# A second drain on GpSimd's queue, behind its last transfer, in a copy kernel

## The chip, the cores and the metric

The kernel runs on one core of a Trainium2 chip. The metric is the device time of one execution in microseconds (us), and lower is better. Three executions of the kernel before took 744.84, 744.95 and 745.9 us; their median, 744.95 us, is the time before.

Three of the core's engines matter here, and they matter through their queues of instructions: SyncE (SP in the profile), ScalarE (ACT) and GpSimd (POOL). Each of them issues DMA transfers. TensorE and VectorE (PE, DVE) have no work but to take part in the barriers at the two ends of the program. A name with a q behind it (POOLq, SPq) means an instruction that the engine's sequencer handles, such as a wait, a semaphore update or a drain.

## The reference

The reference cuts overlapping windows out of each sequence of a batch. Nothing is computed: every output element is a copy of an input element.

```python
batch, length, dim = x.shape                      # 32, 4096, 256, float32
n_windows = (length - window_size) // stride + 1  # 64, 32 -> 127
for i in range(n_windows):
    start = i * stride
    result[:, i] = x[:, start:start + window_size].copy()
```

The output is (32, 127, 64, 256) float32. Since the stride is half the window, each block of 32 rows (32 x 256 floats, 32 KB) goes to two places: it is the first half of one window and the second half of the window before it.

## The kernel before

The kernel is made of DMA transfers alone. The program calls a 32 KB block `blk`; a sequence has 128 of them, and 127 windows of two blocks.

There are two ways for a sequence. Eleven of the 32 (every third, from the second on) are *staged* by `Staging`: ScalarE's queue loads the 128 blocks into a tile in SBUF, one block for each partition, and stores the tile twice, once to the first halves of the windows and once to the second halves. There are six tiles; six sequences are loaded and stored, and then the other five use the same tiles again. The other 21 sequences are *direct*: transfers from DRAM to DRAM copy 16 windows at a time, issued by SyncE's queue (`windows`, line 34 in the profile). Whether a turn is one transfer of 1 MB or two of 512 KB is settled by the sum kept in `share`.

What is left over are the `edges`: 15 windows at one end of each direct sequence (4 for the last one), that don't fill a block of 16. GpSimd's queue issues them. It first waits on the semaphore `near` (line 192), which one of SyncE's last transfers raises, and then, for each edge, for the stores of the staged neighbours in `place` (lines 194 to 196). In the trace, 18 of these transfers are issued one after the other from 654.39 us on, and three more from 702.01 us. Behind them, line 200 issues one last transfer of GpSimd by `columns` (line 44 in the profile): nine windows of sequence 30, cut into sixteenths of a block so that it consists of 4 KB pieces. Then SyncE waits for the stores of the last staged sequence, and issues a small transfer of the same kind (line 202), at 729.80 us.

The semaphores `done`, `near`, `rest` and `ended` count what has landed. SyncE's queue waits for each of them in lines 204 and 205; GpSimd's transfers of lines 197 and 200 are counted in `rest`. No line of the kernel makes GpSimd wait for its own transfers.

All of this stands inside one `with tc.tile_critical()` (line 172). When that block is left, the program appends instructions of its own, shown under line 172: SyncE raises a semaphore; SyncE, ScalarE and GpSimd each run a DRAIN that waits for it and raises a semaphore in turn; and SyncE waits for these three before it goes on. At the end of the whole program (line 236, where the `TileContext` is left) there follow two barriers over all five engines, again made of DRAIN and EVENT_SEMAPHORE instructions, with a clearing of the semaphores on GpSimd's queue between them.

The instructions of one queue are handled in the order in which they stand in it. The queue of GpSimd from line 200 on therefore reads: the last transfer, the DRAIN of line 172, the instructions of line 236.

Of the kernel before, what the change touches and what calls it, by code (L numbers as in the profile page):

```python
# [125 lines left out]
@with_exitstack  # L126
def kernel(
    ctx: ExitStack,
    tc: tile.TileContext,
    x: bass.AP,  # L130
    window_size: bass.AP,
    stride: bass.AP,
    out: bass.AP,
):
    nc = tc.nc
    W, S = int(window_size), int(stride)
    B, L, D = x.shape
    n_win = (L - W) // S + 1
    assert out.shape == (B, n_win, W, D)
    c = Copier(x, out, B, L, D, W, S, n_win)  # L140


    staged = [*range(1, B, 3)]
    items = [(b, -1 if b == B - 1 else 0, c.nb) for b in staged]
    place = {b: g for g, (b, _, n) in enumerate(items) if n == c.nb}
    direct = [b for b in range(B) if b not in staged]
    pool = ctx.enter_context(tc.tile_pool(name="xb", bufs=1))
    st = Staging(c, tc, pool, x.dtype, items, 6)
    ring_d, ring_s, ring_r = nc.sync, nc.scalar, nc.gpsimd
    done = tc.alloc_semaphore("done")  # L150
    near = tc.alloc_semaphore("near")
    rest = tc.alloc_semaphore("rest")
    total = {done: 0, near: 0, rest: 0}

    def count(dma, sem):
        dma.then_inc(sem, 16)
        total[sem] += 16

    sixteens = []
    for b in direct:
        w = 15 if b - 1 in staged else 0
        sixteens += [(b, w + 16 * j) for j in range((c.nw - w) // 16)]
    singles = [(B - 1, c.nw - 1, 1)]
    edges = [(b, 0 if b - 1 in staged else 112, 15) for b in direct[:-1]]
    last = B - 2
    edges.append((last, 112, 4))

    first_loads, loads, stores = 6 * 17, 5 * 17, 6 * 34  # L170
    turns = share = 0
    with tc.tile_critical():  # L172
        st.run(ring_s)

        for i, (b, w) in enumerate(sixteens):
            sem = near if i == len(sixteens) - 2 else done
            second = turns - first_loads - stores
            loading = turns < first_loads or 0 <= second < loads
            share += 120 if turns < 16 or -8 <= second < 16 else 90 if loading else 18
            if share >= 120:  # L180
                share -= 120
                turns += 4
                count(c.windows(ring_d, b, w, 16, 0), done)
                count(c.windows(ring_d, b, w, 16, 1), sem)
            else:
                turns += 3
                count(c.windows(ring_d, b, w, 16), sem)
            if i == len(sixteens) // 2:
                for b, w, half in singles:
                    count(c.windows(ring_d, b, w, 1, half, 2048), done)  # L190

        ring_r.wait_ge(near, 16)
        for b, w, n in edges:
            for k in (b - 1, b + 1):
                if k in place and b != last:
                    st.wait_stored(ring_r, place[k])
            count(c.windows(ring_r, b, w, n), rest)


        count(c.columns(ring_r, last, 116, 9), rest)  # L200
        st.wait_stored(ring_d, place[B - 1])
        count(c.columns(ring_d, last, 125, 2), done)
        total[st.ended] = st.count[st.ended]
        for sem, n in total.items():
            ring_d.wait_ge(sem, n)
# [35 lines left out]
```

## Time and profile before

| what | value |
|---|---|
| median of three executions | 744.95 us (744.84 to 745.9) |
| profiled execution: its time, from its first to its last instruction | 749.4 us (no other figure is given for it) |
| that span over the median | 4.45 us, 0.6% |
| bytes moved by DMA, mean rate | 313.26 MB, 418 GB/s |
| transfers issued by SyncE, ScalarE, GpSimd | 204, 41, 22 |
| busy time of GpSimd | 12.8 us of 749.4 |
| issue of GpSimd's last transfer | 703.7 us, lasting 581 ns |
| start of the closing of line 172 | 746.6 us |
| last instruction of the program | 749.4 us |

Times in the profile count from the first instruction. A row of a line's instructions has the engine, the operation and how often it occurs, then the shortest, the median and the longest duration in nanoseconds, and then when the first and the last of them started. A row of waits has who waited, on whom, the time in total, how often, and the longest. A row of windows has the stretch, its length, the busy time of GpSimd with its number of instructions, the granted clock of TensorE, the share of the 16 DMA engines in use, and the rate in GB/s.

### The profile page before, as it was taken

The numbers are of one execution on the slowest core, as the hardware profiler recorded it, in microseconds if no ns is written. First come the engines' busy times: TensorE is split into PE (matmuls) and PEld (weight loads), VectorE is DVE, ScalarE is ACT, GpSimd is POOL, SyncE is SP. The second block draws the span as 40 slices with busy tenths as digits, with TensorE's granted clock in tenths as the row PEclk, the third lists the DMA queues.
The fourth block names the chain that finished last, engine by engine and source line by source line (L and its number), as shares of the span: only waits on it lengthen the run. The fifth ranks groups of instructions, "written<-read, shape, count | busy, mean of one in ns | idle before, by whom it ended". The sixth has DMA issues, their size and how long they took to land.

```text
span 749.4 us, 322 instructions
## 1 busy us (share of the span) xinstructions
POOL 12.8 (2%) x26
## 2 busy tenths in 40 slices
POOL 0000000000000000000000000000000000040100
DMA  8999999999999999999999999999999999999996
GB/s 360 401 427 429 427 429 428 434 423 418 420 424 423 418 424 415 422 427 427 414 427 417 429 432 429 430 422 430 429 423 421 423 421 419 425 426 423 431 409 262
DMA packets 18290, 313.26 MB, mean 418 GB/s; under 512 B 4336, under 2 KB 4336, under 8 KB 4528
## 3 DMA queue, kind: packets, MB, share of 16 engines
q1 hardware_dynamic: 8016, 154.32, 48.8%
q10 hardware_dynamic: 9104, 138.41, 44.0%
q0 software_dynamic: 1168, 20.51, 6.5%
q14 instruction: 2, 0.02, 0.0%
HBM read 220.95 MB, written 267.09 MB: 651 GB/s over the span
## 4 chain that ended last, share of the span: by engine, by line
another core or an unknown queue 92%; POOL 2%; issue 0%; POOLq 0%; SPq 0%
POOL out_dram L34 2%; POOL out_dram L44 0%; POOLq L236 0%; SPq L172 0%; POOLq L114 0%
## 5 line engine op out<-in xcount | busy, mean ns | idle before, releaser
L34 POOL DMA_DIRECT2D out_dram<-in_x_dram x21 | 12.0, 576 | 691.3 <-DMA out_dram<-in_x_dram 654.0
L44 POOL DMA_DIRECT2D out_dram<-in_x_dram x1 | 0.6, 581 | 0.0
L222 POOL MEMSET const-float32-0.0<- 128x1 f32 x1 | 0.1, 98 | 0.2 <-issue 0.2
L222 POOL MEMSET const-bfloat16-1.0<- 128x1 bf16 x1 | 0.1, 101 | 0.0
L222 POOL MEMSET const-float32-1.0<- 128x1 f32 x1 | 0.1, 98 | 0.0
L222 POOL MEMSET const-uint8-127<- 128x1 uint8 x1 | 0.1, 98 | 0.0
## 6 DMA issues: line engine op xcount, KB each, us to landing
out_dram<-in_x_dram SPq DMA_DIRECT2D x92, 1024.0 KB, 100.7
out_dram<-xb ACTq DMA_DIRECT2D x21, 4096.0 KB, 139.7
out_dram<-in_x_dram SPq DMA_DIRECT2D x110, 512.0 KB, 90.3
xb<-in_x_dram ACTq DMA_DIRECT2D x10, 4096.0 KB, 131.4
out_dram<-in_x_dram POOLq DMA_DIRECT2D x20, 960.0 KB, 38.5
xb<-in_x_dram ACTq DMA_DIRECT2D x4, 1024.0 KB, 15.7
out_dram<-xb ACTq DMA_DIRECT2D x2, 1024.0 KB, 113.4
out_dram<-xb ACTq DMA_DIRECT2D x4, 512.0 KB, 96.9
```

The lines of the kernel that those rows point to most:

```text
L34: return q.dma_start(out=self.oap((b * self.nw + w0) * 2 + h, [[2 * blk, n], row]), in_=self.xap(b * self.nb + w0 + h, [[blk, n], row]), m ...
L44: return q.dma_start(out=self.oap((b * self.nw + w0) * 2, [[part, 16], [2 * self.blk, n], row]), in_=self.xap(b * self.nb + w0, [[part, 16 ...
L222: nc = _bacc.Bacc("TRN2", target_bir_lowering=False, num_devices=1)
```

## The change

One instruction is added to GpSimd's queue, between its last transfer (line 200) and whatever the end of the critical block appends. It waits on no semaphore and raises none. Nothing else is changed: the transfers, their order on each queue, and all waits stay.

```diff
         count(c.columns(ring_r, last, 116, 9), rest)
+        ring_r.drain()
         st.wait_stored(ring_d, place[B - 1])
         count(c.columns(ring_d, last, 125, 2), done)
         total[st.ended] = st.count[st.ended]
```

The queue of GpSimd then reads: the last transfer, the new DRAIN, the DRAIN of line 172, the instructions of line 236. The two lines below the new one are SyncE's.

## The prediction

> **What bounds the kernel now.** I read the page first: how busy the DMA engines are and who moves the bytes.
>
> ```profile
> DMA  8999999999999999999999999999999999999996
> ...
> q1 hardware_dynamic: 8016, 154.32, 48.8%
> q10 hardware_dynamic: 9104, 138.41, 44.0%
> q0 software_dynamic: 1168, 20.51, 6.5%
> ```
>
> The 16 DMA engines are busy for 90% or more of every slice but the first and the last, so for some 740 us this is a kernel of DMA rate. GpSimd's transfers are the software_dynamic queue, 6.5% of the engines' time. An instruction that moves no bytes can matter only where the transfers have ended. So I went to the windows of the end:
>
> ```profile
> 735.00:740.00 5.00, 0.00 (x0) 1.00 1.02 426
> 740.00:745.00 5.00, 0.00 (x0) 1.00 0.54 225
> 745.00:749.40 4.40, 0.00 (x0) 1.00 0.01 5
> ...
> 745.50:746.00 0.50, 0.00 (x0) 1.00 0.04 16
> 746.00:746.50 0.50, 0.00 (x0) 1.00 0.00 0
> ```
>
> Nothing is moved after 746.0 us, yet the program ends at 749.4. These last 3.4 us belong to the closing instructions. The chain of waits on the page does not show them (it stops at GpSimd's last issue, 703.7 us), so I asked for the instructions of the two lines that close the program, within this stretch. Line 172 is the end of the critical block:
>
> ```profile
> L172 SPq EVENT_SEMAPHORE  x2: 17/22/28, 746.6 to 746.8; - x2
> L172 ACTq DRAIN  x1: 8/8/8, 746.7 to 746.7; - x1
> L172 POOLq DRAIN  x1: 1865/1865/1865, 746.7 to 746.7; - x1
> L172 SPq DRAIN  x1: 7/7/7, 746.7 to 746.7; - x1
> L172 SPq NOP  x1: 18/18/18, 748.6 to 748.6; - x1
> ```
>
> Three drains start together at 746.7. ScalarE's takes 8 ns, SyncE's 7 ns, GpSimd's 1865 ns, and SyncE's next instruction starts at 748.6, when GpSimd's has ended. Line 236, the end of the program:
>
> ```profile
> L236 POOLq DRAIN  x3: 34/34/88, 748.6 to 749.2; - x3
> L236 SPq DRAIN  x3: 7/7/7, 748.6 to 748.9; - x3
> ```
>
> The same engine drains three times more, in 34, 34 and 88 ns. So GpSimd's drains are not slow as such; the first behind its transfers is. Last, SyncE's waits:
>
> ```profile
> SPq L205 <- DMA out_dram<-in_x_dram: 15.9, 1, 15.9
> SPq L172 <- POOLq L172: 1.7, 1, 1.7
> ```
>
> SyncE stands for 1.7 us on that one drain with no transfer running. That is on the path, without cover.
>
> **The change part by part.** It removes nothing and moves nothing. It adds one DRAIN on GpSimd's queue, behind this issue:
>
> ```profile
> L44 POOL DMA_DIRECT2D out_dram<-in_x_dram x1: 581/581/581, 703.7 to 703.7; - x1
> ```
>
> *The new drain itself.* It starts at 703.7 + 0.58 = 704.3 us. The trace shows no drain of GpSimd with its own transfers in flight, so I bound it: 34 ns from the rows of line 236, 1865 ns from line 172, and, should it be held until the transfers have landed, until 746.3 us (703.7 plus the last transfer's 42.6 us from issue to landing in the list of DMA issues). Queued behind it is only the DRAIN of line 172, which doesn't start before 746.7. Nobody waits for GpSimd in between: SyncE's transfer at 729.8 us is released by ScalarE's stores. So the cover is GpSimd's idle 746.7 - 704.3 = 42.4 us, and the drain costs nothing on the path at 34 or 1865 ns; past 42.4 us, every further microsecond would be paid in full. I take 1865 ns: it is the row nearest in kind, the first drain behind the same 22 transfers.
>
> *The drain of line 172.* It becomes GpSimd's second drain behind its transfers. Its cost lies between 34 ns (the next row of line 236, again a drain with no transfer in front of it) and the 1865 ns of now. I take the lower end: the new instruction is to line 172 what line 172 now is to line 236, the drain before it on the same queue with no work between. At the program's start there is one more GpSimd drain, right behind four memsets, at 184 ns; by that row 1865 - 184 = 1681 ns go, by 34 ns 1865 - 34 = 1831 ns.
>
> *What is late next.* The 1831 ns do not all reach the end. SyncE's own last semaphore wait before the NOP starts at 746.8 us and takes 28 ns, so it can't run its NOP before some 746.85. What it stands on GpSimd is the 1.7 us of the wait row, and that is the most that can go. Drains of 34 or 184 ns from 746.7 on end at 746.7 or 746.9, so both free the 1.7 to within about 0.1 us. The 0.8 us of barriers from 748.6 to 749.4 move ahead as they are.
>
> *The sum.* 0 for the new drain, -1.7 for SyncE's wait: the profiled span 749.4 becomes 747.7. Only the span is known of the profiled execution, 4.45 us above the median of 744.95. I carry the difference over in microseconds, as a closing cost doesn't scale with the rate of the copy: 744.95 - 1.7 = 743.25 us, 0.23% less. A measurement of this kernel can tell about 0.2%, 1.49 us, from no change, so this is just outside.
>
> **A rule against it.** The 1865 ns row contradicts one that the Trainium skill states. VectorE: DVE Perf Modes, section The DRAIN you can't avoid, says that the drains which the program's opening and closing bring take a constant 12 ns or so on all five engines. By that rule the closing drain would have 12 ns to give, and the time would stay at 744.95; by the row it is 743.25. ScalarE's and SyncE's 8 and 7 ns come near the rule, GpSimd's do not, and the row decides. A second page bears on what the 1865 ns are. PSUM — Partial Sum Buffer, section Engine vs sequencer instructions, says that a drain waits for the engine to go fully idle. Here the engine's last listed work ended at 704.3 and the drain at 746.7 still took 1865 ns, so if the rule holds, something that the profile doesn't list as busy is left over.
>
> **The rivals.**
>
> *It does nothing: the work of the drain arises only once the transfers have landed.* If 1865 ns is for cleaning up completed transfers, the new drain at 704.3 finds almost none completed (the last four were issued within the 2.3 us before it, with medians of 36.9 to 42.6 us to landing), returns early, and line 172 pays 1865 ns again: 744.95 us. Likewise if the price comes from GpSimd's long idleness, as 42 us precede line 172 either way. Against the latter: the transfer issue after an idle 37.4 us started 0.28 us behind its release. For the former I see no row; nothing in the trace separates work left by the issue from work left by the landing.
>
> *Held until the landing, paid once.* If the new drain waits for the transfers and then works, it ends at 746.3 + 1.87 = 748.2, and line 172 adds 0.03. Now line 172's drain ends at 746.7 + 1.87 = 748.5. The gain shrinks to 0.3 us: 744.65.
>
> *Slower: held until the landing, and paid twice.* The same hold, but the price belongs to each drain that follows a long stretch: 748.2 + 1.87 = 750.0 against 748.5, so +1.5 us, 746.45. It decides from the point at which the new drain ends later than 746.7, that is, lasts over 42.4 us. Against it: the three drains of line 236, each right behind another, at 34 to 88 ns. For it only that no row shows a drain over transfers in flight.
>
> **How the numbers follow.** The likeliest, the work moved under the transfers, has 0.70: the drains of line 236 show that a drain leaves little to the next. Doing nothing has 0.14, held and paid once 0.05, held and paid twice 0.11. The predicted time is 743.25. Two of the three runs lie within 0.11 us, the third 0.95 above; with such scatter in both medians, some 0.65 us either way, the likeliest case's own range is 742.6 to 743.9, and about 0.56 of its 0.70 lies beyond 0.2%, 0.14 within. Faster: 0.56. Within 0.2%: 0.14 + 0.14 + 0.05 - 0.01 = 0.32, where the 0.01 is for a do-nothing case with a high reading. Slower: 0.11 + 0.01 = 0.12. The range starts a little under the likeliest case, at 742.5, and ends at 745.6, above the do-nothing case with its scatter; it leaves out the case paid twice and the outermost readings of the others, under 0.2 together.
>
> **What would show it.** In the profile after: a GpSimd DRAIN of a new line at about 704.3 us, of some 1.9 us; line 172's GpSimd DRAIN near 34 to 184 ns; SyncE's wait on GpSimd under line 172 gone or below 0.2 us; the NOP about 0.2 us behind the other drains rather than 1.9; and the stretch from line 172 to the end at some 1.1 us instead of 2.8. The last landing should stay where it is against the span of its run. I would be wrong if line 172 still shows 1865 ns (nothing moved), if the new drain lasts some 42 us (held), or if the rate in the windows from 704 us to 740 falls below the 411 to 431 GB/s that they have now (ten-microsecond windows from 700 to 730): then the drain works at the expense of the transfers, which I gave no case of its own, since 4% of those 42 us would be needed to eat the gain.

## The result, and the profile after

The changed kernel takes 743.55 us (median of 16 executions, 742.88 to 744.21); the kernel before, timed beside it, 744.98 us (16 executions, 743.78 to 746.22). The ratio is 0.9981, 95% interval 0.9973 to 0.9988: faster by 0.19%, 1.4 us, with an interval of 0.9 to 2.0 us. That the time is unchanged is excluded by the interval. The 0.2% that the prediction used as its bound lies inside the interval.

The first line of the page of the changed kernel, and its costliest group:

```profile
span 742.1 us, 323 instructions
...
L34 POOL DMA_DIRECT2D out_dram<-in_x_dram x21 | 12.0, 575 | 685.4 <-DMA out_dram<-in_x_dram 648.7
```

The profiled execution took 743.86 us, so 1.8 us lie around its span. Its span is 7.3 us below that of the profile before, but most of this is not the change. The same group in the page of the kernel before:

```profile
L34 POOL DMA_DIRECT2D out_dram<-in_x_dram x21 | 12.0, 576 | 691.3 <-DMA out_dram<-in_x_dram 654.0
```

GpSimd's first transfer waited 654.0 us before and 648.7 us now, so 5.3 us were gone long before the new instruction was reached: the profile before is of an execution that copied more slowly. The two traces are therefore compared from the last landing on.

The instructions of line 172 in the closing of the changed kernel:

```profile
L172 SPq EVENT_SEMAPHORE  x2: 17/22/28, 740.5 to 740.6; - x2
L172 ACTq DRAIN  x1: 8/8/8, 740.5 to 740.5; - x1
L172 SPq DRAIN  x1: 7/7/7, 740.6 to 740.6; - x1
L172 POOLq DRAIN  x1: 41/41/41, 741.1 to 741.1; - x1
L172 SPq NOP  x1: 18/18/18, 741.2 to 741.2; - x1
```

GpSimd's drain takes 41 ns here instead of 1865. But it starts at 741.1, half a microsecond behind SyncE's and ScalarE's, where the three started together before. The line of the new instruction (201) says why:

```profile
L201 POOLq DRAIN  x1: 43501/43501/43501, 697.6 to 697.6; - x1
```

The new drain lasts 43.5 us, from 697.6 to 741.1. GpSimd's last transfer and its time to landing, in the answer on line 44:

```profile
L44 POOL DMA_DIRECT2D out_dram<-in_x_dram x1: 581/581/581, 697.9 to 697.9; - x1
...
DMA to landing us min/median/max: 42.3/42.3/42.3
```

It landed at 697.9 + 42.3 = 740.2 us. So the new drain was held over the whole flight and ended 0.9 us behind the landing. SyncE's waits in the changed kernel:

```profile
SPq L172 <- POOLq L172: 0.5, 1, 0.5
```

SyncE still stands on GpSimd, for 0.5 us where it was 1.7. That is a saving of 1.2 us. The stretch from the last landing to the last instruction agrees: 749.4 - 746.3 = 3.1 us before, 742.1 - 740.2 = 1.9 us after.

Nothing shows that the transfers paid for the held drain: GpSimd's last one took 42.6 us from issue to landing before and 42.3 us with the drain beside it. The prediction named a fall of the copying rate below 411 to 431 GB/s as a sign against it. These are the windows from 700 to 730 us in the changed kernel:

```profile
700.00:710.00 10.00, 0.00 (x0) 1.00 1.03 428
710.00:720.00 10.00, 0.00 (x0) 1.00 0.99 413
720.00:730.00 10.00, 0.00 (x0) 1.00 1.01 406
```

The 406 is under the 411, but this trace is 6 us nearer to its last landing at the same time. In windows that lie equally far from the last landing, the kernel before has 431, 423 and 411 GB/s, this trace 436, 421 and 406, and a second trace of the changed kernel 434, 413 and 415. The rate is not steadily lower with the drain.

### The profile page after: what moved, and what is told of

Its sections match the earlier page's. It is cut to its first block, busy times and chain, and to the rows that moved or that the text cites. A ratio compares the mean times of both kernels' runs of the same rounds, so it can differ in the third digit from the quotient of the medians.

```text
span 742.1 us, 323 instructions
## 1 busy us (share of the span) xinstructions
POOL 12.7 (2%) x26
## 3 DMA queue, kind: packets, MB, share of 16 engines
q0 software_dynamic: 1168, 20.51, 6.6%
## 4 chain that ended last, share of the span: by engine, by line
another core or an unknown queue 92%; POOL 2%; issue 0%; POOLq 0%; SPq 0%
POOL out_dram L34 2%; POOLq L201 0%; POOLq L237 0%; SPq L172 0%; POOLq L114 0%
## 5 line engine op out<-in xcount | busy, mean ns | idle before, releaser
L34 POOL DMA_DIRECT2D out_dram<-in_x_dram x21 | 12.0, 575 | 685.4 <-DMA out_dram<-in_x_dram 648.7
```

Of the source, the lines that this page charges most:

```text
L34: return q.dma_start(out=self.oap((b * self.nw + w0) * 2 + h, [[2 * blk, n], row]), in_=self.xap(b * self.nb + w0 + h, [[blk, n], row]), m ...
```

## The experiments

They ran on chips on which the kernel before took 752 to 755 us rather than 745, so only ratios to that kernel on the same chip and durations inside a trace are compared. All kernels do the whole copy. Where a landing is given to 0.01 us, it is read from the semaphore records of the trace.

The question after the result: what are the 1865 ns, why did only some of them go, and would they go altogether?

### What the drain's price counts: four transfers, 43 transfers, smaller packets

Three kernels without an early drain change what stands in front of line 172's drain. The first leaves GpSimd four transfers and has SyncE issue the other 18:

```diff
+        ring_d.wait_ge(near, 16)
         ring_r.wait_ge(near, 16)
-        for b, w, n in edges:
+        for i, (b, w, n) in enumerate(edges):
+            q, sem = (ring_d, done) if i < 18 else (ring_r, rest)
...
-                    st.wait_stored(ring_r, place[k])
-            count(c.windows(ring_r, b, w, n), rest)
+                    st.wait_stored(q, place[k])
+            count(c.windows(q, b, w, n), sem)
```

> Only the last four transfers are GpSimd's; the 18 before are issued by SyncE instead, and there is no early drain. Theory A (the drain goes through GpSimd's landed transfers one by one, 1865 ns / 22 = 85 ns each): the drain of line 172 takes some 340 to 500 ns. Theory B (a fixed price of the first drain behind transfers, whatever their number): 1800 to 1900 ns. Theory C (by packets: 1865 ns / 1168 packets of GpSimd's queue): by the packets that the queue then has, a third to a half of 1865 ns.

Line 172's GpSimd drain in that kernel:

```profile
L172 POOLq DRAIN  x1: 395/395/395, 750.9 to 750.9; - x1
```

The second issues each edge as its two halves, 43 transfers in all:

```diff
-            count(c.windows(ring_r, b, w, n), rest)
+            for half in (0, 1):
+                count(c.windows(ring_r, b, w, n, half), rest)
```

> Each of GpSimd's 21 edge transfers is issued as two, one for each half of the windows: 43 transfers of the same bytes and the same data packets, no early drain. Theory A (by transfers): line 172's GpSimd drain takes 43 x 85 = some 3600 ns. Theory B (fixed): 1800 to 1900 ns. Theory C (by packets): nearly as B, 1865 ns times (1168 + 21 x 16)/1168 = 2400 ns, if the packets that raise the semaphore count.

```profile
L172 POOLq DRAIN  x1: 3580/3580/3580, 750.8 to 750.8; - x1
```

The third keeps 22 transfers and cuts the edges into 8 KB pieces:

```diff
-            count(c.windows(ring_r, b, w, n), rest)
+            count(c.windows(ring_r, b, w, n, None, 8192), rest)
```

> The same 22 transfers, but the 21 edge transfers are cut into pieces of 8 KB instead of 32 KB, so that the queue has several times the packets; no early drain. Theories A (by transfers) and B (fixed): line 172's GpSimd drain stays at 1800 to 1900 ns. Theory C (by packets): it grows with the packets of GpSimd's queue, to some 4000 to 5000 ns. The issue of each transfer may take longer.

GpSimd's DMA queue (packets, MB, share) and line 172's GpSimd drain in the kernel with small pieces, from two views:

```profile
q0 software_dynamic: 3184, 20.52, 7.5%
```

```profile
L172 POOLq DRAIN  x1: 1865/1865/1865, 758.9 to 758.9; - x1
```

With 2.7 times the packets (3184 for 1168) the drain takes the same 1865 ns to the nanosecond. With the number of transfers it goes in a straight line: (3580 - 1865) / 21 = 81.7 ns for each one above 22, (1865 - 395) / 18 = 81.7 ns for each one below, and 395 - 4 x 81.7 = 68 ns where the line would meet no transfer. Theory A stands: from four to 43 transfers the drain takes **68 ns plus 82 ns for each transfer that GpSimd has issued**. (A drain with none in front of it is not on the line: the second one behind the change took 41 ns.) A fixed price and a price by packets are out, and so is one by bytes, as the 43 transfers carry the same 20.5 MB as the 22. Each transfer raises its semaphore 16 times in every one of these traces, so whether the drain counts transfers or these signals stays open. The times of these kernels (one execution each: 753.95, 757.09 and 763.41 us, where before took 751.96) are no measure of the drain, since the copying itself changed: GpSimd's transfers landed at 744.6, 750.4 and 758.5 us in their traces.

### An early drain that isn't the last

```diff
             count(c.windows(ring_r, b, w, n), rest)
+            if b == edges[17][0]:
+                ring_r.drain()
```

> The new drain stands behind GpSimd's 18th transfer instead of the last, four transfers before the end of its queue. If a drain is held until the transfers in front of it have landed, it lasts from about 664 to over 730 us, the last four are issued only then, and the program ends 0 to 4 us later. Theory A (by transfers): line 172's drain has four left, 340 to 500 ns. Theory B (fixed, again for each drain that has transfers in front of it): 1800 to 1900 ns; B with a price paid only once in the program: under 200 ns.

The new drain (line 199), and then line 172's, in that kernel:

```profile
L199 POOLq DRAIN  x1: 71121/71121/71121, 663.8 to 663.8; - x1
```

```profile
L172 POOLq DRAIN  x1: 385/385/385, 748.3 to 748.3; - x1
```

The drain is held for 71 us, until 0.79 us behind the landing of the 18 transfers in front of it (734.17 us), and GpSimd issues its last four only then. The program was expected to end 0 to 4 us later for it; by one execution each it did not (751.38 us, where before took 751.96), and the late four landed within 8.0 to 10.7 us. Line 172's drain has four left and takes 385 ns, near the 395 of a kernel that has four in all. So a drain takes its transfers off the account of the next one, and the price is paid neither again in full nor once in the program.

### A second drain, but behind the landing

```diff
         count(c.columns(ring_r, last, 116, 9), rest)
+        ring_r.wait_ge(rest, total[rest])
+        ring_r.drain()
```

> A second drain as in the change, but GpSimd first waits until all its transfers have landed. Theory A (what the change saves is the going through transfers while others still fly): the new drain starts within 0.1 us of the last landing and takes 68 + 22 x 82 = 1865 ns, line 172's drain 34 to 41 ns, and SyncE waits some 1.3 us on it, as the list is gone through from about 0.3 us earlier than before. A rival by which any drain ahead of SyncE's signal saves what the change saves: the new drain takes under 1 us, SyncE waits 0.5 us.

The new drain (line 202), and SyncE's wait on line 172's:

```profile
L202 POOLq DRAIN  x1: 1865/1865/1865, 747.6 to 747.6; - x1
```

```profile
SPq L172 <- POOLq L172: 1.4, 1, 1.4
```

It starts behind the last landing (747.60 us), takes the whole 1865 ns, and SyncE waits 1.4 us, only 0.3 less than before. A second drain as such saves nothing but its earlier start; standing over the transfers while they fly saves the rest, 0.9 us.

### What is left behind the landing: 43 and four transfers with the early drain

The changed kernel's drain ended 0.95 us behind the landing (741.09 against 740.14). Is this a fixed time, or does it too count transfers? The kernels with 43 and with four transfers, each with the line of the change:

```diff
         count(c.columns(ring_r, last, 116, 9), rest)
+        ring_r.drain()
```

> 43 transfers of GpSimd, as before with each edge in two halves, and the early drain behind the last. Theory A1 (the held drain takes off each transfer as it lands, and has only the last ones left): it ends 0.8 to 1.1 us behind the last landing, as with 22. Theory A2 (behind the last landing it goes through what is left in a time that grows with the number of transfers, 0.95 us for 22): 1.7 to 2.0 us behind it. Line 172's drain takes 34 to 50 ns in both.

> Four transfers of GpSimd, the 18 before issued by SyncE, and the early drain behind the last. Theory A1: the drain ends 0.8 to 1.1 us behind GpSimd's last landing, as with 22 or 43. Theory A2: 0.1 to 0.4 us behind it. Line 172's drain takes 34 to 50 ns in both, and SyncE doesn't wait for it, as ScalarE's stores land later.

The new drain with 43 transfers (line 202) and SyncE's wait on line 172's:

```profile
L202 POOLq DRAIN  x1: 54012/54012/54012, 699.7 to 699.7; - x1
```

```profile
SPq L172 <- POOLq L172: 1.4, 1, 1.4
```

It ends at 753.69 us, 1.81 us behind the last landing at 751.88. The new drain with four transfers (line 203):

```profile
L203 POOLq DRAIN  x1: 37701/37701/37701, 704.9 to 704.9; - x1
```

It ends at 742.60 us, 0.22 us behind GpSimd's last landing at 742.38, and SyncE has no wait on line 172's drain any more, since ScalarE's stores land 7 us later. Theory A2 holds: what a held drain leaves behind the landing grows with the number of transfers, by (1.81 - 0.22) / 39 = 0.041 us each, from 0.06 us for none. The line gives 0.95 for 22 and 0.79 for 18, as measured. So **an early drain takes half of the 82 ns off the path for each transfer, and the other half is still left behind the landing**, in each of the traces with a held drain. Which work the two halves are, no run here tells.

### Taking GpSimd's transfers out of the end

If what remains is tied to GpSimd's own landings, it goes when these come before the others'. The last transfer of GpSimd is moved to SyncE, first without the early drain, then with it:

```diff
-        count(c.columns(ring_r, last, 116, 9), rest)
+        count(c.columns(ring_d, last, 116, 9), done)
         st.wait_stored(ring_d, place[B - 1])
```

```diff
             count(c.windows(ring_r, b, w, n), rest)
+        ring_r.drain()
...
-        count(c.columns(ring_r, last, 116, 9), rest)
+        count(c.columns(ring_d, last, 116, 9), done)
```

> GpSimd's last transfer (line 200) is issued by SyncE instead, at the end of its windows and ahead of its wait; no early drain. GpSimd keeps 21 transfers. Theory A (the drain costs about 68 ns plus 82 ns for each transfer of GpSimd since its last drain, the line through 4, 22 and 43 transfers): line 172's GpSimd drain takes 68 + 21 x 82 = 1790 ns, SyncE waits some 1.6 us on it, and the time stays within 1 us of before, up or down by where the moved transfer lands. A rival by which the drain waits for the engines' last data (and not through a list) expects less than 1 us, as GpSimd's transfers have landed some us before the others.

> As the run with the last transfer moved to SyncE, and in addition the early drain behind GpSimd's last edge transfer. Theory A (the early drain is held until GpSimd's own transfers have landed, and ends under 1 us behind them): GpSimd's transfers land before ScalarE's last stores, so the drain is over before the closing, line 172's drain takes 34 to 70 ns, SyncE's 0.5 us wait that the changed kernel has left is gone, and the time is 0.4 to 0.6 us below the changed kernel, some 1.7 to 2 us below before. A rival by which the drain is held for all queues' transfers leaves the 0.5 us wait: the changed kernel's time.

Line 172's GpSimd drain without the early drain:

```profile
L172 POOLq DRAIN  x1: 1783/1783/1783, 749.8 to 749.8; - x1
```

It starts 2.1 us behind GpSimd's last landing (747.74 us) and still takes what the line gives for 21 transfers, 68 + 21 x 81.7 = 1784 ns: the price doesn't fade by itself once the transfers have landed. The ratio to before is 1.0003, 0.9989 to 1.0017. With the early drain, the new drain (line 198) and line 172's:

```profile
L198 POOLq DRAIN  x1: 39912/39912/39912, 708.7 to 708.7; - x1
```

```profile
L172 POOLq DRAIN  x1: 41/41/41, 750.2 to 750.2; - x1
```

The drain ends at 748.59 us, 0.91 us behind GpSimd's last landing (747.68) and ahead of ScalarE's last store (749.92). SyncE has no wait on GpSimd left in the closing. The ratio to before is 0.9977, 0.9967 to 0.9987.

The third way is that GpSimd issues nothing, and SyncE issues all its transfers with the same waits:

```diff
-        ring_r.wait_ge(near, 16)
+        ring_d.wait_ge(near, 16)
...
-                    st.wait_stored(ring_r, place[k])
-            count(c.windows(ring_r, b, w, n), rest)
+                    st.wait_stored(ring_d, place[k])
+            count(c.windows(ring_d, b, w, n), rest)
-        count(c.columns(ring_r, last, 116, 9), rest)
+        count(c.columns(ring_d, last, 116, 9), rest)
```

> All of GpSimd's transfers are issued by SyncE, at the end of its queue, with the same waits; GpSimd issues none and there is no early drain. Theory A: line 172's drain takes 34 to 200 ns and the closing is 1.7 us shorter than before. What two queues in place of three do to the copying itself is open: between 2 us less and 5 us more; so the time lies between 741.5 and 748.5 where before is 745.

In that kernel line 172 has no GpSimd drain at all, and the closing shows SyncE's instructions close together:

```profile
L172 SPq EVENT_SEMAPHORE  x2: 17/17/17, 749.6 to 749.8; - x2
...
L172 SPq NOP  x1: 18/18/18, 749.8 to 749.8; - x1
```

From the last landing (749.41 us) to the last instruction (750.70) it takes 1.3 us, where before took 3.1. Its ratio to before is 0.998, 0.9968 to 0.9992. The changed kernel was timed on the same chip:

> The changed kernel once more, on the chip of the other three runs, as their measure. Theory A: its early drain ends 0.5 to 1.2 us behind GpSimd's last landing, SyncE's wait on line 172's drain is 0.2 to 0.7 us, and it is 1.0 to 1.7 us faster than before.

Its waits show the same 0.5 us on line 172's drain, its new drain ends 0.96 us behind the last landing (750.21 against 749.25), and its ratio to before is 0.9976, 0.9961 to 0.9991. The two kernels that have no wait left are not faster than the changed kernel by anything that these intervals could show: the medians on this chip are 753.14 (changed), 753.04 (last transfer moved, early drain) and 752.86 (no transfer of GpSimd). The 0.4 to 0.6 us below the changed kernel that had been expected of the kernel with the moved transfer and the early drain did not show. The half microsecond of the wait is below what this timing resolves, and no version here is shown to beat the change.

## Why the prediction was right or wrong

The time was right: 743.55 measured, 743.25 predicted, well inside the range. So was the sign, and the place. Most of the chance, 0.56, went to a gain of over 0.2%; the median's 0.19% falls in the 0.32 for within it, and the interval covers both sides. The mechanism was not right: the prediction gave a new drain of some 42 us as a sign of being wrong, and the new drain lasted 43.5. That the time came so near all the same is in part luck. With the 1.2 us that the traces show in place of the 1.7, the sum gives 743.75 us, and the measured interval of 0.9 to 2.0 us can't tell the two apart. Step by step:

- **Where the time lies: right.** The 1865 ns of one drain, with no transfer running, were on the path, and the change shortened this stretch, from 3.1 us behind the last landing to 1.9.
- **The new drain itself: the step that failed.** I took 1865 ns at 704.3 us, by the first drain behind the same transfers; it lasted 43,501 ns. The row that I chose was of a drain whose transfers had all landed, and the held drain, which I named as a bound, was what happened. Nor does it start where the issue in front of it ends, as I had added up: its row begins 0.3 us before that issue's (697.6 against 697.9), and 1.6 us before the 18th issue's in the kernel with the drain in the middle (663.8 against 665.4). The cover that I put at 42.4 us, here 740.5 - 697.6 = 42.9, was overrun by 0.6 us: that is the 0.5 us which SyncE still waits.
- **The drain of line 172: right.** 41 ns, between the 34 and the 184 that I gave.
- **What is late next: wrong as a consequence.** I had SyncE's own instructions late next, and so the full 1.7 us gone. It is the new drain's end, and the term is 1.2 us. The measured time moved by 1.4 us, with an interval that holds both.
- **The rivals.** The change is closest to "held until the landing, paid once", which I gave 0.05 and priced at a gain of 0.3 us, as I had the full price fall due behind the landing. The hold was right and the price was half: 0.95 us rather than 1.87. That gives 0.3 + 0.9 = 1.2 us. "It does nothing" falls with line 172's 41 ns, and "paid twice" with it. Against the measured 1.2 us of this term, the likeliest case's 1.7 was 0.5 too high, and the rival's 0.3 was 0.9 too low.
- **The two rules of the Trainium skill.** VectorE: DVE Perf Modes, section The DRAIN you can't avoid, has boilerplate drains of the preamble and postamble at a constant 12 ns or so on all five engines. I read this as a rule for the drains under lines 172 and 236, which the page does not say; GpSimd's drain of line 172 took 385 to 3580 ns where transfers stood in front of it. PSUM — Partial Sum Buffer, section Engine vs sequencer instructions, has a drain wait for the engine to go fully idle; on GpSimd this takes in the transfers that it issued, by the 43.5 us with no other work listed behind the issue, and by the kernel whose held drain ended behind GpSimd's own landing and ahead of ScalarE's last store. I had the second rule in hand and drew from it only that something was left over, not that the new drain would wait for it.

## What to carry to other kernels

Where GpSimd issues transfers, look at its drain in the closing of the program: here each transfer of GpSimd cost 82 ns at the end of the program, at 128 to 960 KB, and still 6.3 us behind the last of their landings in the kernel with four. An early drain takes half of this off the path as long as nothing that must be issued stands behind it, and all of it if GpSimd's transfers land far enough ahead of the last ones of the other queues (2.2 us here, where the drain had 0.9 us left). Fewer transfers on that queue shorten the drain too, and none leave nothing to wait for; with four, no run shows that the program got faster. And when an added wait is priced, ask first what it waits for: a row of the same instruction with nothing in flight says little of it over 42 us of transfers.

## What the runs showed of the hardware

Three things I had not expected. A DRAIN on GpSimd behind transfers is held until they have landed, 43.5 us here and 71.1 us in the kernel with the drain in the middle. Its price, behind the landing, is a straight line in the number of transfers since the last drain, 395, 1783, 1865 and 3580 ns for 4, 21, 22 and 43, and it was the same 1865 ns with 1168 packets and with 3184. And of this price a drain that was already standing when the transfers landed pays half, 0.22, 0.79, 0.91, 0.95 and 1.81 us behind the landing for 4, 18, 21, 22 and 43.
